# Pairing the recurrence's matmul batches and moving copies and scalings to ScalarE in a two-layer RWKV-7 / Mamba-2 / MoE kernel

## The chip, the core and the metric

The kernel runs on one core of a Trainium2 chip. The metric is the device time of one execution in microseconds (us); a lower time is better. Before the change three runs gave 3489.57 us as their median (3477.48 to 3494.5).

Engines are named as the profile names them: PE is TensorE's matmul, PEld its weight load, DVE is VectorE, ACT is ScalarE, POOL is GpSimd, SP is SyncE, which issues nearly all DMAs.

## What is computed

Two layers over 256 latent and 256 context tokens of width 1024. Each layer has a mixing block and a mixture of experts. The mixing block is one projection whose columns go to an RWKV-7 branch (16 heads of 64, scanned in both directions), a Mamba-2 branch (8 groups of 4 heads, both directions) and two gates. The two places that the change touches come from these lines of the reference:

```python
def step(S, inp):                       # RWKV-7, one token, one direction
    r_t, w_t, k_t, v_t, a_t, b_t = inp
    sa = jnp.einsum("bhij,bhj->bhi", S, a_t)
    S = S * w_t[:, :, None, :] + sa[..., None] * b_t[:, :, None, :] + v_t[..., None] * k_t[:, :, None, :]
    y = jnp.einsum("bhij,bhj->bhi", S, r_t) if emit else None
...
y = y.reshape(bsz, -1, SSM_INNER) * jax.nn.silu(z.astype(F32))     # Mamba-2, the end of a group
yg = y.reshape(bsz, -1, SSM_GROUPS, SSM_INNER // SSM_GROUPS)
yg = yg * lax.rsqrt(jnp.mean(yg * yg, axis=-1, keepdims=True) + SSM_NORM_EPS)
y = (yg.reshape(bsz, -1, SSM_INNER) * norm_w).astype(out_dtype)
```

The mixture of experts picks two of 32 experts for each token; its code is not changed.

## The kernel before

Everything that a layer does is first recorded as a list of operations. A planner inside the kernel then writes out the order in which they are issued: it keeps a clock for each engine, a price for each operation, a due time for each stream of work and a count of buffer slots, and at each step takes the operation that can start earliest, the most urgent first. What it emits is one fixed order for each engine; on the chip each engine works through its own order and waits, where an operand is not there yet, with all that stands behind. So any edit can move instructions far away from it.

The mixing block of a layer runs three kinds of streams at once: eight head pairs of the RWKV branch, eight groups of the Mamba branch, and gates. The large projections (tiles `mm` and `psz`) are split into a high and a low 16-bit half of the weights (`wh`, `wl`), which ACT and DVE make.

The RWKV recurrence is done in chunks of 64 tokens. For a head pair `i` and a direction `d`:

- `rw_dir` makes the chunk factors. `psg` holds products of keys, from which DVE masks out `QA` and `AR`. Two batches of 16 matmuls of 64x64 follow: `psat` transposes `Z`, and `psav` multiplies `QA` with the values in `SU`. ACT copies `psat` to `Z`. The two halves of `psav` go to `SU`, one by ACT, one by DVE. `Z`, `SU`, `XT` and `AR` are then written to DRAM (`sd`), because each has two slots.
- `rw_solve` inverts the triangular factors on DVE (`slW`, `slY`, `slM`) and gives `TT`; `psW` and `psZ` are its matmuls.
- `rw_chain` comes one head pair later. It reads `Z`, `SU`, `XT` and `AR` back from DRAM into the same slots and runs four batches: `psta` (`TT` times `Z`), `psua` (`TT` times `SU`), `psgt` and `psra` (with the new `Z`). Then come `psH` (state of each chunk, from `SU`, then a chain of seven steps through `GT` and `St`) and `psY` (the output).

A batch is recorded by `batch` as one operation of 16 matmuls that stay together (`together`), since they use the PE array as 64x64 tiles and other matmuls use it as 128x128. PSUM tiles of these batches come from a tag with two slots.

`ssm_group` ends with the normalisation: `yg` (128 tokens x 256 columns) is multiplied by the reciprocal root `rr` on DVE, transposed on PE into `psyT`, scaled by ACT into `yt`, and split by DVE into two 16-bit halves in `smo`, which are written to DRAM.

All instructions stand at line 683 in the profile (the planner's emitter), so they are told apart by their tiles.

Of the kernel before, what the change touches and what calls it, by code (L numbers as in the profile page):

```python
# [12 lines left out]
F32 = mybir.dt.float32  # L13
# [3 lines left out]
AF = mybir.ActivationFunctionType  # L17
OP = mybir.AluOpType
# [3 lines left out]
NT = 512  # L22
# [664 lines left out]
class Kernel:  # L687
# [469 lines left out]
    def rw_dir(self, l, i, d, S, kk, w0):  # L1157
        nc, wk, rp = self.nc, self.wk, self.rp
# [41 lines left out]
        for e in range(2):  # L1200
            rows = slice(64 * e, 64 * e + 64)
# [41 lines left out]

        rows = self.rows2
        SU = S["SU"][d]
        ps = self.batch("psat", lambda c, e: Z[rows[e], c, 0], lambda c, e: self.ident[rows[e], 64 * e:64 * e + 64])
        A.activation(Z[:, :, 0], ps, AF.Copy)
        ps = self.batch("psav", lambda c, e: QA[rows[1 - e], 2 * c + e], lambda c, e: SU[rows[1 - e], c, e])
        A.activation(SU[rows[0], :, 0], ps[rows[0]], AF.Copy)
        V.tensor_copy(SU[rows[1], :, 1], ps[rows[1]])  # L1250
        sd = self.sd[:, i, d]
        nc.sync.dma_start(sd[:, 0], Z.rearrange("p c b t -> p (c b t)"))
        nc.sync.dma_start(sd[:, 1], SU.rearrange("p c b t -> p (c b t)"))
# [7 lines left out]

    def batch(self, name, lhs, rhs, cs=range(8)):

        ps = self.psum("g", [128, 8, 64], name)
        with self.nc.together():
            for c in cs:
                for e in range(2):
                    self.nc.tensor.matmul(ps[self.rows2[e], c], lhs(c, e), rhs(c, e), start=True, stop=True)
        return ps

    def rw_solve(self, i):

# [80 lines left out]
    def rw_chain(self, l, i):  # L1353

        nc, wk, rp = self.nc, self.wk, self.rp
        V, A, T, G = nc.vector, nc.scalar, nc.tensor, nc.gpsimd
        S = self.pair[i]
        full = l == 0  # L1360
        c0 = 0 if full else 4
        o0 = 64 * c0
        E = range(2)
        rows = (slice(0, 64), slice(64, 128))
        seq = [[0, 1, 2, 3, 4, 5, 6, 7], [3, 2, 1, 0, 7, 6, 5, 4]]
        py = S["py"] = self.psum("y", [128, NT], "psY", bufs=1)
        yo = lambda c, e: py[rows[e], 64 * c - o0:64 * c - o0 + 64]
        GT = wk.tile([128, 2, 8, 64], F32, name="GT")
        St = wk.tile([128, 2, 8, 64], F32, name="St", tag="X")
        PH = []  # L1370
        batch = self.batch
        for d in range(2):
            TT = S["TT", d]
            sd = self.sd[:, i, d]
            Z = S["Z", d] = rp.tile([128, 8, 2, 64], F32, name="Z", bufs=4)
            nc.sync.dma_start(Z.rearrange("p c b t -> p (c b t)"), sd[:, 0])
            SU = rp.tile([128, 8, 2, 64], F32, name="SU", bufs=4)
            nc.sync.dma_start(SU.rearrange("p c b t -> p (c b t)"), sd[:, 1])
            XT = rp.tile([128, 8, 128], F32, name="XT", bufs=4)
            nc.sync.dma_start(XT.rearrange("p c t -> p (c t)"), sd[:, 2])  # L1380
            AR = rp.tile([128, 16, 64], F32, name="AR", bufs=4)
            nc.sync.dma_start(AR[:, 2 * c0:].rearrange("p c t -> p (c t)"), sd[:, 3, 128 * c0:])
            mid = seq[d][1:7]

            ps = batch("psta", lambda c, e: TT[rows[e], c], lambda c, e: Z[rows[e], c, 0])
            A.activation(Z[:, :, 0], ps, AF.Copy)
            ps = batch("psua", lambda c, e: TT[rows[e], c], lambda c, e: SU[rows[e], c, e])
            A.activation(SU[rows[0], :, 0], ps[rows[0]], AF.Copy)
            V.tensor_copy(SU[rows[1], :, 1], ps[rows[1]])
            ps = batch("psgt", lambda c, e: Z[rows[e], c, 0], lambda c, e: XT[rows[e], c, 64 * e:64 * e + 64], mid)  # L1390
            for cs in ((slice(0, 3), slice(5, 8)) if d else (slice(1, 7),)):
                n = cs.stop - cs.start
                V.tensor_tensor(GT[:, d, cs], ps[:, cs], self.id2[:, None, :].to_broadcast([128, n, 64]), op=OP.add)
            ph = self.psum("c", [128, 8, 64], "psH")
            PH.append(ph)
            with nc.together():
                for n, c in enumerate(seq[d][:7]):
                    for e in E:
                        T.matmul(ph[rows[e], c], XT[:, c, 64 * e:64 * e + 64], SU[:, c, e], start=n == 0, stop=False,
                                 skip_group_check=True)  # L1400
            ps = batch("psra", lambda c, e: Z[rows[e], c, 0], lambda c, e: AR[rows[e], 2 * c + e], range(c0, 8))
            V.tensor_tensor(Z[:, c0:, 1], Z[:, c0:, 1], ps[:, c0:], op=OP.add)
            with nc.together():
                for c in range(c0, 8):
                    for e in E:
                        T.matmul(yo(c, e), SU[:, c, e], AR[:, 2 * c + e], start=not d and c == c0, stop=False,
                                 skip_group_check=True)
        for n in range(7):
            cs = [seq[d][n] for d in range(2)]
            if n:  # L1410
                with nc.together():
                    for d, c in enumerate(cs):
                        for e in E:
                            T.matmul(PH[d][rows[e], c], GT[rows[e], d, c], St[rows[e], d, c], start=False, stop=True,
                                     skip_group_check=True)
            for d, c in enumerate(cs):
                nx, pl = seq[d][n + 1], S["pl", d][:, c:c + 1]
                if d:
                    A.activation(St[:, d, nx], PH[d][:, c], AF.Copy, scale=pl)
                else:  # L1420
                    V.tensor_scalar(St[:, d, nx], PH[d][:, c], pl, None, op0=OP.mult)
        with nc.together():
            for d in range(2):
                for c in range(c0, 8):
                    if c != seq[d][0]:
                        for e in E:
                            T.matmul(yo(c, e), St[rows[e], d, c], S["Z", d][rows[e], c, 1], start=False, stop=True,
                                     skip_group_check=True)
# [71 lines left out]
    def ssm_group(self, l, g):  # L1500
# [104 lines left out]
        rr = wk.tile([128, 4], F32, name="yrr", bufs=2)  # L1605
        self.rsqrt(rr[:, t0:], ss[:, t0:], 4 - t0)
        for t in range(t0, 4):
            V.tensor_scalar(yg[:, t], yg[:, t], rr[:, t:t + 1], None, op0=OP.mult)
        for b in range(2):
            pt = self.psum("t", [128, NT], "psyT")  # L1610
            for t in range(t0, 4):
                T.transpose(pt[:, 128 * t:128 * t + 128], yg[:, t, 128 * b:128 * b + 128], self.ident)
            j = 2 * g + b
            nw = self.nws[:, j:j + 1]
            yt = wk.tile([128, NT], F32, name="yt", bufs=2)
            A.activation(yt[:, o0:], pt[:, o0:], AF.Copy, scale=nw)
            o = wk.tile([128, 2, NT], F16, name="smo", bufs=2)
            V.tensor_copy(o[:, 0, o0:], yt[:, o0:])
            V.tensor_tensor(o[:, 1, o0:], yt[:, o0:], o[:, 0, o0:], op=OP.subtract)
            nc.sync.dma_start(self.smd[:, j, :, o0:], o[:, :, o0:])  # L1620


# [589 lines left out]
```

## Time and profile before

| | before |
|---|---|
| median of three runs | 3489.57 us (3477.48 to 3494.5) |
| the profiled execution | 3486.93 us |
| its span, first to last instruction | 3484.8 us |
| PE busy | 3117.4 us (89%) |
| DVE busy | 2418.7 us (69%) |
| ACT busy | 1725.3 us (50%) |
| POOL busy | 773.3 us (22%) |
| mean granted TensorE clock | 0.942 |

The page's slices show the stages: mixing of layer 0 up to 1143 us, its merge and routing, experts of layer 0 from about 1370 to 1909 us, mixing of layer 1 from there to 2848 us, merge, and experts of layer 1 to the end. The profile counts a PE that has matmuls in flight as busy, so a busy share near 90% can still hold pauses of some hundred nanoseconds. A wait is listed with the engine or DMA whose event came last before the waiting instruction started.

### The profile page before, as it was taken

The page shows a single profiled execution, that of the slowest core. Times are in us where ns is not written, and L with a number is a line of the kernel's source. Part 1 is how long each engine was busy: PE and PEld are TensorE (multiplying, and loading weights), DVE is VectorE, ACT ScalarE, POOL GpSimd, SP SyncE. Part 2 cuts the span into 40 slices and gives each one's busy share as a digit, 9 for nine tenths or more (in the row PEclk, how much of TensorE's full clock was granted, in tenths as well). Part 3 has the DMA queues.
Part 4 walks back from the last instruction along what each step waited for, and adds up shares of the span by engine and source line. Part 5 has one row for each costly group of instructions (what it writes and reads, how often), then busy time and mean ns, then how long its engine had stood idle before and what let it go on. Part 6 is the DMA issues. An engine that isn't in the chain of part 4 may idle for free. (4 is left out here: it accounts for less than half of the span.)

```text
span 3484.8 us, 84587 instructions
## 1 busy us (share of the span) xinstructions
PE 3117.4 (89%) x34930; PEld 2072.5 (59%) x34930; DVE 2418.7 (69%) x4474; ACT 1725.3 (50%) x3189; POOL 773.3 (22%) x1048
## 2 busy tenths in 40 slices
PE   6899999899889998999998698888888889898887
PEld 3556666566566457888887366566666668333332
DVE  4887877877867347999997788888887765221112
ACT  4554555544544225998886654555544443111111
POOL 1332323333332011111111243334332321000000
PEclk8999999999999997999999798999989999899998
DMA  7243463553355626999996433444234458899996
GB/s 290 91 162 133 157 215 124 199 201 126 141 183 173 249 97 242 408 390 404 394 391 256 178 108 136 150 147 151 96 140 140 156 187 304 340 401 399 401 400 259
DMA packets 283503, 794.49 MB, mean 228 GB/s; under 512 B 31457, under 2 KB 62177, under 8 KB 283105
## 3 DMA queue, kind: packets, MB, share of 16 engines
q1 hardware_dynamic: 278368, 772.17, 60.0%
q10 hardware_dynamic: 3584, 12.58, 0.9%
q8 instruction: 279, 4.57, 0.5%
q0 software_dynamic: 1152, 4.19, 0.3%
q14 instruction: 120, 0.97, 0.1%
HBM read 688.16 MB, written 100.66 MB: 226 GB/s over the span
## 5 line engine op out<-in xcount | busy, mean ns | idle before, releaser
L683 PE MATMUL mm<-h,wh 128*128 128x512 f16 (+1 forms) x2432 | 680.2, 359 | 6.4 <-ACT wh L683 6.3
L683 PEld LDWEIGHTS <-wh 128*128 128x128 f16 x3200 | 306.7, 99 | 261.4 <-issue 24.6
L683 PE MATMUL mm<-h,wl 128*128 128x512 f16 (+2 forms) x1216 | 434.4, 359 | 5.4 <-DVE wl L683 5.3
L683 DVE SCALAR_TENSOR_TENSOR ewl<-est,ewh 128x1024 f16<-128x1024 f32 x352 | 413.0, 1228 | 16.5 <-ACT ewh L683 8.1
L683 ACT ACTIVATE ewh<-est 128x1024 f16<-128x1024 f32 x384 | 380.9, 1050 | 14.1 <-PE pse L683 10.1
L683 DVE SCALAR_TENSOR_TENSOR wl<-wst,wh 128x1024 f16<-128x1024 f32 (+1 forms) x234 | 290.9, 1256 | 36.7 <-ACT wh L683 35.9
L683 PE MATMUL pse<-xg,ewh 128*128 128x96 f16 x4096 | 276.4, 206 | 4.5 <-DVE xg L683 2.1
L683 PEld LDWEIGHTS <-ewh 128*128 128x128 f16 x4096 | 265.6, 98 | 6.9 <-ACT ewh L683 0.9
L683 PE MATMUL pse<-xg,ewl 128*128 128x96 f16 x2048 | 264.4, 206 | 1.0 <-POOL ewl L683 1.0
L683 ACT ACTIVATE wh<-wst 128x1024 f16<-128x1024 f32 (+1 forms) x234 | 239.8, 1043 | 5.9 <-DMA wst<-in_wmix_dram 5.5
L683 PEld LDWEIGHTS <-wl 128*128 128x128 f16 (+1 forms) x1600 | 158.7, 99 | 137.3 <-DVE wl L683 13.0
L683 PE MATMUL pse<-est,xg 128*64 128x512 f32 x512 | 236.6, 598 | 0.0
L683 PE MATMUL pse<-esh,xg 128*64 128x512 f32 x512 | 236.6, 598 | 0.0
L683 PEld LDWEIGHTS <-ewl 128*128 128x128 f16 x2048 | 199.5, 98 | 7.4 <-issue 4.2
L683 DVE SCALAR_TENSOR_TENSOR cva<-cvz,cwh,cva 128x512 f32<-128x512 f32 (+1 forms) x256 | 199.6, 780 | 1.6
L683 POOL TENSOR_TENSOR ewl<-est,ewh 128x1024 f16<-128x1024 f32 x32 | 70.0, 2188 | 488.4 <-ACT ewh L683 429.1
L683 POOL TENSOR_TENSOR sht<-shz 128x512 f32<-128x512 f32 (+3 forms) x56 | 65.6, 1171 | 468.6 <-ACT shz L683 377.7
L683 DVE TENSOR_TENSOR slM<-slY,slW 128x144 f32<-128x144 f32 (+22 forms) x496 | 162.7, 328 | 8.3
L683 DVE SCALAR_TENSOR_TENSOR eyl<-psy,egs,eyh 128x512 f16<-128x512 f32 x32 | 24.0, 751 | 205.5 <-ACT eyh L683 205.5
L683 ACT ACTIVATE eu<-pse 128x384 f32<-128x384 f32 (+1 forms) x64 | 34.5, 540 | 243.4 <-PE pse L683 243.4
L683 DVE TENSOR_REDUCE slY<-slM 128x2 f32<-128x4 f32 (+23 forms) x496 | 147.3, 297 | 7.2
L683 PE MATMUL psz<-wh,h 128*128 128x256 f16 x768 | 150.3, 283 | 0.0
(560 smaller groups left out, 7173.6 us busy)
## 6 DMA issues: line engine op xcount, KB each, us to landing
est<-in_w_dram SPq DMA_DIRECT2D x576, 512.0 KB, 7.1
wst<-in_wmix_dram SPq DMA_DIRECT2D x246, 512.0 KB, 6.3
esh<-in_w_dram SPq DMA_DIRECT2D x384, 256.0 KB, 6.6
wst<-in_wmod_dram SPq DMA_DIRECT2D x96, 512.0 KB, 5.8
sd<-XT SPq DMA_DIRECT2D x32, 512.0 KB, 3.6
sd<-Z SPq DMA_DIRECT2D x32, 512.0 KB, 4.0
sd<-SU SPq DMA_DIRECT2D x32, 512.0 KB, 4.9
XT<-sd SPq DMA_DIRECT2D x32, 512.0 KB, 5.6
```

The lines of the kernel that those rows point to most:

```text
L683: r = getattr(e, m)(*[real(x) for x in a], **{n: real(x) for n, x in k.items()})
```

## The change

Two things are done.

1. A new helper `batches` records two batches as one operation of 32 matmuls. The pairs are `psat` with `psav`, `psta` with `psua`, and `psgt` with `psra`. The operation takes both PSUM slots at once.
2. Work goes from DVE to ACT. The second half of `psav` is copied by ACT; `yg` is scaled by ACT; ACT writes the high half of `smo` straight from `psyT`, and DVE makes the low half from `psyT` in one instruction. `yt` and the 16-bit copy on DVE are gone.

```diff
-        ps = self.batch("psat", lambda c, e: Z[rows[e], c, 0], lambda c, e: self.ident[rows[e], 64 * e:64 * e + 64])
+        ps, pu = self.batches(
+            ("psat", lambda c, e: Z[rows[e], c, 0], lambda c, e: self.ident[rows[e], 64 * e:64 * e + 64], range(8)),
+            ("psav", lambda c, e: QA[rows[1 - e], 2 * c + e], lambda c, e: SU[rows[1 - e], c, e], range(8)))
         A.activation(Z[:, :, 0], ps, AF.Copy)
-        ps = self.batch("psav", lambda c, e: QA[rows[1 - e], 2 * c + e], lambda c, e: SU[rows[1 - e], c, e])
-        A.activation(SU[rows[0], :, 0], ps[rows[0]], AF.Copy)
-        V.tensor_copy(SU[rows[1], :, 1], ps[rows[1]])
+        for e in range(2):
+            A.activation(SU[rows[e], :, e], pu[rows[e]], AF.Copy)
...
+    def batches(self, *sets):
+        out = [self.psum("g", [128, 8, 64], x[0]) for x in sets]
         with self.nc.together():
+            for ps, (_, lhs, rhs, cs) in zip(out, sets):
+                for c in cs:
+                    for e in range(2):
+                        self.nc.tensor.matmul(ps[self.rows2[e], c], lhs(c, e), rhs(c, e), start=True, stop=True)
+        return out
...
-            ps = batch("psta", lambda c, e: TT[rows[e], c], lambda c, e: Z[rows[e], c, 0])
+            ps, pu = self.batches(("psta", lambda c, e: TT[rows[e], c], lambda c, e: Z[rows[e], c, 0], range(8)),
+                                  ("psua", lambda c, e: TT[rows[e], c], lambda c, e: SU[rows[e], c, e], range(8)))
...
-            ps = batch("psgt", lambda c, e: Z[rows[e], c, 0], lambda c, e: XT[rows[e], c, 64 * e:64 * e + 64], mid)
+            ps, pr = self.batches(
+                ("psgt", lambda c, e: Z[rows[e], c, 0], lambda c, e: XT[rows[e], c, 64 * e:64 * e + 64], mid),
+                ("psra", lambda c, e: Z[rows[e], c, 0], lambda c, e: AR[rows[e], 2 * c + e], range(c0, 8)))
...
-            ps = batch("psra", lambda c, e: Z[rows[e], c, 0], lambda c, e: AR[rows[e], 2 * c + e], range(c0, 8))
...
-            V.tensor_scalar(yg[:, t], yg[:, t], rr[:, t:t + 1], None, op0=OP.mult)
+            A.activation(yg[:, t], yg[:, t], AF.Copy, scale=rr[:, t:t + 1])
...
-            yt = wk.tile([128, NT], F32, name="yt", bufs=2)
-            A.activation(yt[:, o0:], pt[:, o0:], AF.Copy, scale=nw)
             o = wk.tile([128, 2, NT], F16, name="smo", bufs=2)
-            V.tensor_copy(o[:, 0, o0:], yt[:, o0:])
-            V.tensor_tensor(o[:, 1, o0:], yt[:, o0:], o[:, 0, o0:], op=OP.subtract)
+            A.activation(o[:, 0, o0:], pt[:, o0:], AF.Copy, scale=nw)
+            V.scalar_tensor_tensor(o[:, 1, o0:], pt[:, o0:], nw, o[:, 0, o0:], op0=OP.mult, op1=OP.subtract)
```

The planner makes a new order of the whole mixing block. PE's order in the mixing block of layer 1, beside the preparation of the seventh head pair, where `psta` of the sixth starts; a row is one run of equal matmuls, `mm` are projections, `LDWEIGHTS` loads a weight tile. Before:

```order
34412 L683 MATMUL psta<-Z,TT 64x64 x16
34413 L683 MATMUL psx<-cst,X 128x128 x8
34414 L683 LDWEIGHTS wl
34415 L683 MATMUL mm<-h_30051,wl 128x256
34416 L683 MATMUL psgt<-XT,Z 64x64 x12
34417 L683 MATMUL psua<-SU,TT 64x64 x16
34418 L683 MATMUL psra<-AR,Z 64x64 x8
```

The same place in the changed kernel:

```order
34450 L683 MATMUL psta<-Z,TT 64x64 x16
34451 L683 MATMUL psua<-SU,TT 64x64 x16
34452 L683 MATMUL psat<-cst,Z 64x64 x16
34453 L683 MATMUL psav<-SU,QA 64x64 x16
34454 L683 MATMUL psH<-SU,XT 64x64 x14
34455 L683 MATMUL psY<-AR,SU 64x64 x8
34456 L683 MATMUL psgt<-XT,Z 64x64 x12
34457 L683 MATMUL psra<-AR,Z 64x64 x8
```

`psx` has moved ahead of `psta`; `psat` and `psav` of the second direction have moved up from behind `psua` of the second direction, and all eight batches now stand in one stretch of 64x64 tiles.

ACT's order at the same head pair, from the copy of `psat` of the first direction on (`wh` is a weight split, `cvt` a convolution of the Mamba branch). Before:

```order
1974 L683 ACTIVATE Z<-psat 128x8x64
1975 L683 ACTIVATE SU<-psav 64x8x64
1976 L683 ACTIVATE Z<-psta 128x8x64
1977 L683 ACTIVATE XT<-psx 128x512 x2
1978 L683 ACTIVATE SU<-psua 64x8x64
1979 L683 ACTIVATE cvt<-cva 128x512
1980 L683 ACTIVATE SU<-psua 64x8x64
```

In the changed kernel:

```order
1975 L683 ACTIVATE Z<-psat 128x8x64
1976 L683 ACTIVATE SU<-psav 64x8x64 x2
1977 L683 ACTIVATE XT<-psx 128x512 x2
1978 L683 ACTIVATE wh<-wst 128x1024
1979 L683 ACTIVATE shz<-mm 128x256
1980 L683 ACTIVATE sht<-sht,muh 128x256
1981 L683 ACTIVATE Z<-psta 128x8x64
1982 L683 ACTIVATE SU<-psua 64x8x64
1983 L683 ACTIVATE Z<-psat 128x8x64
1984 L683 ACTIVATE SU<-psav 64x8x64 x2
```

ACT has the second copy of `psav` too, and other work now stands between these copies and those of `psta` and `psua`.

## Rows read from the trace of the kernel before

**Rows 1.** Windows, mixing of layers 0 and 1: stretch, length, busy us by engine.

```profile
core 0: us, PE busy (x) PEld busy (x) DVE busy (x) ACT busy (x) POOL busy (x), PEclk, DMA share, GB/s
60.00:1143.00 1083.00, 997.54 (x11166) 646.74 (x11162) 847.23 (x1724) 549.60 (x1213) 340.02 (x483) 0.97 0.45 160
...
1909.00:2848.00 939.00, 794.45 (x9216) 575.11 (x9216) 766.46 (x1631) 490.27 (x1049) 307.00 (x481) 0.91 0.41 141
```

**Rows 2.** Timeline of PE near 300 us: start, length, instruction, tiles, count.

```profile
300.31 0.38 PE L683 MATMUL mm<-h,wh 128*128 128x512 f16 x1
300.62 0.45 PE L683 MATMUL psH<-St,GT 64*64 64x64 f32 x8
301.00 0.39 PE L683 MATMUL mm<-h,wl 128*128 128x512 f16 x1
301.23 0.59 PE L683 MATMUL mm<-h,wh 128*128 128x512 f16 x2
```

**Rows 3.** Timeline, layer 1, seventh head pair: a batch pair, its write and reload.

```profile
2644.09 0.97 PE L683 MATMUL psat<-cst,Z 64*64 64x64 f32 x26
...
2645.93 0.39 PE L683 MATMUL mm<-h,wh 128*128 128x256 f16 x2
...
2646.82 0.58 ACT L683 ACTIVATE SU<-psav 64x512 f32<-64x512 f32 x1
...
2647.45 0.37 SPq L683 DMA_DIRECT2D sd<-Z  x1
...
2647.88 0.42 SPq L683 DMA_DIRECT2D Z<-sd  x1
...
2648.39 0.99 SPq L683 DMA_DIRECT2D sd<-SU  x1
...
2649.43 0.47 SPq L683 DMA_DIRECT2D SU<-sd  x1
...
2654.06 1.98 PE L683 MATMUL psta<-Z,TT 64*64 64x64 f32 x32 [3.81 <-DMA Z<-sd]
```

**Rows 4.** Windows: the stretch that begins with that `psta`.

```profile
2653.50:2660.30 6.80, 6.24 (x83) 5.74 (x85) 1.50 (x4) 1.69 (x3) 0.00 (x0) 0.50 0.49 196
```

**Rows 5.** Groups of DVE by form: count, busy us, mean ns, idle before.

```profile
L683 DVE SCALAR_TENSOR_TENSOR eyl<-psy,egs,eyh 128x512 f16<-128x512 f32 x32 | 24.0, 751 | 205.5 <-ACT eyh L683 205.5
...
L683 DVE COPY SU<-psav 64x512 f32<-64x512 f32 x32 | 22.2, 694 | 7.3 <-PE psav L683 3.3 <-ACT SU L683 3.1
L683 DVE TENSOR_SCALAR yg<-yg,yrr 128x256 f32<-128x256 f32 x48 | 14.7, 355 | 9.3 <-POOL yrr L683 9.3
...
L683 DVE TENSOR_TENSOR smo<-yt,smo 128x512 f16<-128x512 f32 x16 | 11.7, 732 | 0.3
...
L683 DVE CAST smo<-yt 128x512 f16<-128x512 f32 x16 | 6.8, 426 | 27.0 <-ACT yt L683 27.0
L683 DVE CAST smo<-yt 128x256 f16<-128x256 f32 x16 | 6.6, 411 | 2.9 <-ACT yt L683 2.7
```

**Rows 6.** Groups of ACT by form, the same columns.

```profile
L683 ACT ACTIVATE St<-psH,pl 128x64 f32<-128x64 f32 x112 | 35.3, 316 | 109.0 <-PE psH L683 108.9
L683 ACT ACTIVATE zz<-yg 128x256 f32<-128x256 f32 x48 | 20.1, 418 | 31.5 <-DVE yg L683 29.8 <-DVE st L683 1.4
...
L683 ACT ACTIVATE SU<-psav 64x512 f32<-64x512 f32 x32 | 18.7, 585 | 15.4 <-PE psav L683 13.3 <-DVE SU L683 2.0
```

**Rows 7.** Groups of PE that wait for the batches' operands, the same columns.

```profile
L683 PE MATMUL psta<-Z,TT 64*64 64x64 f32 x1024 | 43.9, 244 | 23.7 <-DMA Z<-sd 22.6 <-DVE Sst L683 0.5 <-issue 0.4
...
L683 PE MATMUL psua<-SU,TT 64*64 64x64 f32 x1024 | 40.3, 235 | 14.8 <-DMA SU<-sd 12.5 <-DVE slM L683 1.7 <-DVE cva L683 0.4
...
L683 PE MATMUL psH<-SU,XT 128*64 128x64 f32 x896 | 36.8, 226 | 11.6 <-DVE SU L683 7.5 <-ACT SU L683 4.1
```

**Rows 8.** DMA issues: tiles, count, KB each, median us to landing.

```profile
Z<-sd SPq DMA_DIRECT2D x32, 512.0 KB, 6.2
SU<-sd SPq DMA_DIRECT2D x32, 512.0 KB, 7.2
```

More of the change, by code (lines that the diff above doesn't have):

```diff
@@ L1262, in batch @@
     def batch(self, name, lhs, rhs, cs=range(8)):
-        ps = self.psum("g", [128, 8, 64], name)
+        return self.batches((name, lhs, rhs, cs))[0]
+    def batches(self, *sets):
+        out = [self.psum("g", [128, 8, 64], x[0]) for x in sets]
         with self.nc.together():
[L1266 to L1269, printed above, removed]
+            for ps, (_, lhs, rhs, cs) in zip(out, sets):
[3 more added lines that the diff above has]
+        return out
     def rw_solve(self, i):
@@ L1370, in rw_chain @@
         PH = []
-        batch = self.batch
         for d in range(2):
@@ L1383, in rw_chain @@
             mid = seq[d][1:7]
-            ps = batch("psta", lambda c, e: TT[rows[e], c], lambda c, e: Z[rows[e], c, 0])
+            ps, pu = self.batches(("psta", lambda c, e: TT[rows[e], c], lambda c, e: Z[rows[e], c, 0], range(8)),
+                                  ("psua", lambda c, e: TT[rows[e], c], lambda c, e: SU[rows[e], c, e], range(8)))
             A.activation(Z[:, :, 0], ps, AF.Copy)
-            ps = batch("psua", lambda c, e: TT[rows[e], c], lambda c, e: SU[rows[e], c, e])
-            A.activation(SU[rows[0], :, 0], ps[rows[0]], AF.Copy)
-            V.tensor_copy(SU[rows[1], :, 1], ps[rows[1]])
-            ps = batch("psgt", lambda c, e: Z[rows[e], c, 0], lambda c, e: XT[rows[e], c, 64 * e:64 * e + 64], mid)
+            A.activation(SU[rows[0], :, 0], pu[rows[0]], AF.Copy)
+            V.tensor_copy(SU[rows[1], :, 1], pu[rows[1]])
+            ps, pr = self.batches(
+                ("psgt", lambda c, e: Z[rows[e], c, 0], lambda c, e: XT[rows[e], c, 64 * e:64 * e + 64], mid),
+                ("psra", lambda c, e: Z[rows[e], c, 0], lambda c, e: AR[rows[e], 2 * c + e], range(c0, 8)))
             for cs in ((slice(0, 3), slice(5, 8)) if d else (slice(1, 7),)):
@@ L1400, in rw_chain @@
                                  skip_group_check=True)
-            ps = batch("psra", lambda c, e: Z[rows[e], c, 0], lambda c, e: AR[rows[e], 2 * c + e], range(c0, 8))
-            V.tensor_tensor(Z[:, c0:, 1], Z[:, c0:, 1], ps[:, c0:], op=OP.add)
+            V.tensor_tensor(Z[:, c0:, 1], Z[:, c0:, 1], pr[:, c0:], op=OP.add)
             with nc.together():
```

## The prediction

> **What bounds the kernel now.** I read the windows by stage first. The edits lie in the mixing blocks alone, which fill 1083 and 939 us of the span [rows 1]; the experts and merges have other code, and I leave them as they are. In the mixing of layer 0 PE is busy 997.5 of 1083 us (92%) and DVE 847.2 (78%): PE sets the pace and only some 85 us of its idle time can be won. In layer 1 PE is busy 794.5 of 939 us (85%) and DVE 766.5 (82%): neither engine is full, both run through fixed orders, and each waits for the other, so that relief of DVE can show there. ACT is busy for 51% and 52% and POOL for about a third. The granted clock is 0.97 and 0.91, so layer 1 also spends a part of its time at the lower of the two levels, 1.2 GHz.
>
> Then I read one place. In layer 1, PE ran out of work and waited 3.81 us for the reload of `Z` before `psta` [rows 3]. The stretch that began with that `psta` had a granted clock of 0.50, the 1.2 GHz level, for 6.8 us [rows 4]. So a stall of some microseconds costs its own length and then about half of the next 6.8 us. Over the whole kernel PE idled 23.7 us before `psta`, 14.8 before `psua` and 11.6 before `psH` on its first inputs, 50.1 us together, nearly all for the two reloads and the two copies into `SU` [rows 7].
>
> **Fewer changes of the array's tiling.** Pairing lets the planner put 64x64 batches next to each other. Counted over PE's whole order up to the merges, neighbours of unlike tile size fall from 469 to 441 in layer 0 and from 327 to 272 in layer 1: 83 changes, 41 round trips. The price of a trip: from one 512-column `mm` to the next are 0.23 us (301.00 to 301.23), with a step of `psH` between them 0.69 us (300.31 to 301.00), so that step costs 0.46 us for its 8 records [rows 2]. In a long stretch `psat` and `psav` take 2645.93 - 2644.09 = 1.84 us for 64 records, 0.23 us for 8 [rows 3]. The difference, 0.23 us, is a round trip. 41 x 0.23 = 9 us, on PE and so on the path: **-9 us**. The trip is the same whatever else happens; only the count could mislead, where a change fell into an idle moment (bounds 0 and -9).
>
> Not all pairs are new. Before, `psat` and `psav` were already neighbours 26 times of 32, `psgt` and `psra` 22 times, `psta` and `psua` 3 times. So the change of order is mostly in the last pair, and the trips come from there.
>
> **Work off DVE.** Away go 32 copies of `psav` (22.2 us), 48 scalings of `yg` (14.7 us) and 32 casts (6.8 and 6.6 us): 50.3 us [rows 5]. The subtraction turns from two SBUF operands into one from PSUM with a scale; the nearest row is `eyl`, 751 ns against 732 ns for the subtraction now, so that is free. By layer: layer 0 has 16 copies, 32 scalings and the wide casts, 11.1 + 9.8 + 6.8 = 27.7 us; layer 1 the remaining 22.6 us. How much comes through lies between nothing (DVE's idle time just grows) and all 50.3 us. For layer 0 I take a fifth, 6 us, since PE is 92% busy there; for layer 1 half, 11 us, as PE and DVE are almost equally loaded. **-17 us**.
>
> **Work onto ACT.** 32 copies of 585 ns are 18.7 us. The scaling of `yg` has no row; `zz<-yg`, the same 128x256 with SBUF on both sides, takes 418 ns, `St<-psH` with a scale per partition but 64 columns 316 ns [rows 6]. I take 418 ns, the row of the same size: 48 x 0.418 = 20 us. The write of `smo` takes the place of that of `yt`. So ACT has 39 us more on top of 550 and 490 us [rows 1]. It idles half of the time, which hides most of it. Not hidden is where a copy is waited for: `SU` of `psav` was done by two engines side by side and now by one, 585 ns later; who waits is the write `sd<-SU`, but that stood behind `sd<-Z` and `Z<-sd` on SP's queue until 2648.39, 1 us after ACT's copy had ended at 2647.40 [rows 3]. I take **+4 us**, between 0 and 39.
>
> Here a rule speaks against the change. `yg` costs 355 ns on DVE and by the nearest row 418 ns on ACT [rows 5, 6], so in engine time the move loses. The Trainium skill's page "ScalarE: Activation LUTs", section "Rules for kernel authors", says that multiplications and the like belong on VectorE, not on ScalarE, since VectorE does them faster per element. The trace agrees on the price and by that rule this term would be a loss; what it leaves out is that DVE is the fuller engine here.
>
> **The pairs' own waits.** A pair is placed where both inputs are there. `psH` used to stand right behind `psua`, `psra` or a few projections; now, at the place shown from the order, `psat` and `psav` lie between (1.84 us [rows 3]) and a copy takes 585 to 694 ns [rows 5, 6]. I take half of the 11.6 us: **-6 us**. The reloads can go both ways. `psua` now follows `psta` at once, so PE waits for the later of `Z` and `SU`: `SU<-sd` is issued 1.55 us after `Z<-sd` [rows 3] and takes 7.2 us against 6.2 [rows 8], some 2.5 us later. Against that the planner has put more in front: at the place of the 3.81 us stall the order has 26 projections, two halves of `psg` and the `psx` set between `psav` and `psta`, before 17 projections and one half. The bounds are the whole 35 us of waits for reloads (22.6 + 12.5 [rows 7]) won, and 32 x 2.5 = 80 us lost; I take **0**.
>
> **Sum.** -9 - 17 + 4 - 6 = -28 us. The profiled execution took 3486.93 us (span 3484.8 us and 2.1 us around it), so 3459 us; the median of the runs is 2.6 us above it, so 3462 us. A measurement of this kernel tells about 0.5% from no change, 17 us: faster is below 3472 us, slower above 3507 us.
>
> **Rivals.**
>
> *PE has no room, and DVE's relief stays slack.* For it: 92% busy in layer 0, and the waits that the edits touch are 50.1 us in both layers [rows 7], of some 230 us in which PE idles in the two mixing blocks [rows 1]. Then only the trips and ACT's 4 us remain: 3490 - 9 + 4 = 3485 us, no change. Chance 0.26.
>
> *Slower: the pair waits for `SU`.* PE's order is fixed, so `psta` and all projections behind `psua` stand until `SU` has landed. For it: the two reloads go through one queue, one behind the other [rows 3]. Against it: more work in front. It decides from the point where the work between `psav` and `psua` is shorter than the way of `SU` through DRAM: from the end of its copy at 2647.40 to 2649.43 + 7.2 = 2656.6, some 9 us. If half of the 32 places fall short by 2.5 us, that is 40 us, and if every second of those brings 6.8 us at half clock, 8 x 3.4 = 27 us more: 3490 + 67 - 28 = 3529 us. Chance 0.15.
>
> *Slower: ACT's copies come too late.* As a mechanism of this kernel: ACT's queue is in order, so `Z<-psta` stands behind the scalings and PE stands at `psgt`; all 39 us on the path and DVE's relief lost gives 3490 - 9 - 6 + 39 = 3514 us. For it: `Z<-psta` now has a weight split and two shifts ahead of it. Against it: ACT is idle half of the time. This is the outcome of the rule on ScalarE cited above. Chance 0.05.
>
> *Much faster: the stalls fall together.* All 50.3 us off DVE count, the 9 us of trips, 12 us of waits before `psH` and a third of the reloads' 35, without stretches at half clock behind them: 3490 - 83 = 3407 us. For it: the clock of 0.91 in layer 1. Chance 0.12.
>
> **How the numbers follow.** My forecast, 3462 us, has 0.42. Faster is forecast and much faster, 0.54; the same 0.26; slower 0.20. The likeliest case alone spans 3435 to 3472 us. The range for 8 in 10 must take in no change and parts of both tails: 3415 to 3515 us.
>
> **What would show it.** Layer 0's mixing, which ends with the first `psbr`, should be about 12 us shorter than now, and layer 1's some 16 us shorter than 939 us [rows 1]. DVE should be about 28 and 23 us less busy in the two stretches, ACT some 20 us more in each. The idle time before `psta` should stay near 24 us with `psua` near zero, and that before `psH` halve. If `psua` shows long waits for `SU<-sd`, the second rival is right; if ACT's copy of `psta` ends `psgt`'s waits, the third. Wrong altogether would be the sum if unrelated waits (projections for their weights, `pscw` for the decay) change by more than these terms, because the planner has moved everything.

## The result, and the profile after the change

Six runs of the changed kernel gave a median of 3442.36 us (3439.25 to 3446.36); six runs of the kernel before beside them 3484.45 us. The ratio is 0.9879 [0.9865, 0.9893]: **42 us faster**, where 28 us were forecast. The profiled execution took 3439.67 us (span 3437.7 us, mean granted clock 0.942, as before).

By stage, with the first `psbr` as the end of a mixing block:

| stage, us | before | after | difference | forecast |
|---|---|---|---|---|
| to the first `psbr` of layer 0 | 1143.7 | 1125.3 | -18.4 | -12 |
| merge and routing, layer 0 | 226.1 | 217.5 | -8.6 | |
| experts, layer 0 | 530.4 | 529.9 | -0.5 | |
| mixing, layer 1 | 947.6 | 924.2 | -23.4 | -16 |
| merge, layer 1 | 133.0 | 133.6 | +0.6 | |
| experts, layer 1 | 504.1 | 507.1 | +3.0 | |

The 8.6 us of the first merge belong at least in part to the mixing before it: the trace has 11551 matmuls ahead of the first `psbr` now and 1221 in the merge, where it had 11471 and 1299, so some 80 were brought forward. Nothing else moved by more than 3 us.

Windows of the kernel after, one for each mixing block (start and end, length, busy time and instructions of PE, PEld, DVE, ACT, POOL, granted clock, DMA share, GB/s); they answer to [rows 1]:

```profile
60.00:1125.00 1065.00, 990.74 (x11242) 646.89 (x11240) 826.35 (x1662) 570.76 (x1262) 346.06 (x481) 0.97 0.46 165
1882.00:2797.00 915.00, 785.18 (x9199) 574.19 (x9200) 738.89 (x1584) 507.56 (x1078) 295.04 (x481) 0.90 0.42 146
```

The length less PE's busy time is PE's idle time: 74 and 130 us, against 85 and 145 before. DVE has 21 and 28 us less to do, ACT 21 and 17 us more. The clock stayed where it was.

The groups of the edited instructions and of those that wait for them (busy us, mean ns, idle us before them and what ended it):

```profile
L683 PE MATMUL psua<-SU,TT 64*64 64x64 f32 x1024 | 39.9, 232 | 10.7 <-DMA SU<-sd 10.5
L683 PE MATMUL psta<-Z,TT 64*64 64x64 f32 x1024 | 39.8, 230 | 10.6 <-DMA Z<-sd 9.4 <-ACT xT L683 0.7 <-POOL rwq L683 0.4
L683 ACT ACTIVATE SU<-psav 64x512 f32<-64x512 f32 x64 | 37.6, 588 | 2.4 <-PE psav L683 1.9
...
L683 PE MATMUL psH<-SU,XT 128*64 128x64 f32 x896 | 35.2, 229 | 7.4 <-ACT SU L683 5.3 <-DVE SU L683 1.9
...
L683 DVE COPY SU<-psua 64x512 f32<-64x512 f32 x32 | 22.2, 695 | 13.6 <-PE psua L683 8.4 <-ACT SU L683 3.2 <-DMA wst<-in_wmix_dram 1.3
...
L683 ACT ACTIVATE yg<-yg,yrr 128x256 f32<-128x256 f32 x48 | 20.9, 497 | 11.3 <-POOL yrr L683 11.3
```

Against [rows 7], the idle time before `psta` fell from 23.7 to 10.6 us, before `psua` from 14.8 to 10.7, before `psH` from 11.6 to 7.4. The scaling of `yg` costs ACT 497 ns, more than the 418 ns assumed from [rows 6]. DVE's new subtraction costs what was assumed from [rows 5]:

```profile
L683 DVE SCALAR_TENSOR_TENSOR smo<-psyT,nws,smo 128x512 f16<-128x512 f32 x16 | 12.0, 750 | 48.7 <-ACT smo L683 48.7
```

Last, what PE waits for from the first mixing block to the second merge (us in total, times, longest us):

```profile
PE psW L683 <- DVE slO L683: 25.5, 10, 4.2
PE pstr L683 <- DVE rmss L683: 21.2, 1, 21.2
PE psx L683 <- POOL X L683: 16.5, 8, 3.0
PE pscw L683 <- ACT lp L683: 11.9, 8, 3.2
PE pspos L683 <- DVE at L683: 11.1, 1, 11.1
PE psua L683 <- DMA SU<-sd: 10.5, 9, 2.7
PE psx L683 <- DVE X L683: 10.5, 8, 2.6
```

The reload of `Z`, the longest wait before the change (22.6 us), is gone from the top, and the longest now is for DVE's triangular solve (`slO`): 25.5 us, where the same row had 12.9 us before:

```profile
PE psW L683 <- DVE slO L683: 12.9, 7, 2.6
```

### The profile page after: what moved, and what is told of

Read it like the earlier page. It is cut to its first block, busy times and chain, and to the rows that moved or that the text cites. A ratio compares the mean times of both kernels' runs of the same rounds, so it can differ in the third digit from the quotient of the medians.

```text
span 3437.7 us, 84603 instructions
## 1 busy us (share of the span) xinstructions
PE 3098.2 (90%) x34930; PEld 2068.0 (60%) x34930; DVE 2371.8 (69%) x4362; ACT 1762.4 (51%) x3269; POOL 768.1 (22%) x1048
## 3 DMA queue, kind: packets, MB, share of 16 engines
q1 hardware_dynamic: 278368, 772.17, 60.6%
## 5 line engine op out<-in xcount | busy, mean ns | idle before, releaser
L683 POOL TENSOR_TENSOR rmsr<-rmss,mhalf 128x1 f32<-128x1 f32 x16 | 12.7, 793 | 576.3 <-DVE rmss L683 568.4
```

Source lines behind the costliest of these rows:

```text
L683: r = getattr(e, m)(*[real(x) for x in a], **{n: real(x) for n, x in k.items()})
```

## The experiments

The times are medians of several runs beside runs of the kernel before on the same chip; the ratio is to that kernel (its medians were 3484 to 3487 us). Two such medians differ by chance by some 7 us, as the intervals show. "After" is the changed kernel, 3442 us.

### Which half of the change counts

The moves to ACT alone, in the order that the planner makes of them:

```diff
-        V.tensor_copy(SU[rows[1], :, 1], ps[rows[1]])
+        A.activation(SU[rows[1], :, 1], ps[rows[1]], AF.Copy)
...
-            V.tensor_scalar(yg[:, t], yg[:, t], rr[:, t:t + 1], None, op0=OP.mult)
+            A.activation(yg[:, t], yg[:, t], AF.Copy, scale=rr[:, t:t + 1])
...
-            A.activation(yt[:, o0:], pt[:, o0:], AF.Copy, scale=nw)
             o = wk.tile([128, 2, NT], F16, name="smo", bufs=2)
-            V.tensor_copy(o[:, 0, o0:], yt[:, o0:])
-            V.tensor_tensor(o[:, 1, o0:], yt[:, o0:], o[:, 0, o0:], op=OP.subtract)
+            A.activation(o[:, 0, o0:], pt[:, o0:], AF.Copy, scale=nw)
+            V.scalar_tensor_tensor(o[:, 1, o0:], pt[:, o0:], nw, o[:, 0, o0:], op0=OP.mult, op1=OP.subtract)
```

> The moves from VectorE to ScalarE alone, no pairs; the planner makes its own order. Before is 3484 us and the changed kernel 3442 us here, 42 us apart. Theory of the sum (relief of DVE and fewer tiling trips are separate terms): relief and ScalarE's extra work were -13 of -28 us, so about half of the 42 us shows: some 3464 us, with 50 us less DVE time and 39 us more ACT time. Rival, the pairs are all of it: 3480 to 3488 us. Rival, the relief is all of it: 3440 to 3448 us.

Measured: 3455.81 us, 0.991 [0.9893, 0.9928], so -30 us: more than the sum said (3464), less than the rival in which the relief is all of it.

The three pairs alone: the changed kernel with these lines turned back.

```diff
-        for e in range(2):
-            A.activation(SU[rows[e], :, e], pu[rows[e]], AF.Copy)
+        A.activation(SU[rows[0], :, 0], pu[rows[0]], AF.Copy)
+        V.tensor_copy(SU[rows[1], :, 1], pu[rows[1]])
...
-            A.activation(yg[:, t], yg[:, t], AF.Copy, scale=rr[:, t:t + 1])
+            V.tensor_scalar(yg[:, t], yg[:, t], rr[:, t:t + 1], None, op0=OP.mult)
...
```

> The three pairs alone, with the copies, scalings and casts on VectorE as before. Theory of the sum: trips and waits before psH were -15 of -28 us, so some 3464 us; PE's tiling changes in the mixing blocks are 713 here too (432 + 281), which at 0.23 us a round trip is 9 us. Rival, the pairs are all of it: 3440 to 3448 us. Rival, the relief is all of it: 3480 to 3488 us.

Measured: 3480.44 us, 0.9977 [0.9966, 0.9989], so -5 us by the medians and -8 us by the ratio. The moves bring the larger part; with both the gain is 42 us, not far from the sum of the two, 35 to 38 us. That both also change the order is the trouble with these two runs, and the reason for the next two.

### The engine or the order

An added field lets the planner price an instruction on one engine while it is issued on the other at the same place, so that order and engine can be changed apart. The copies of `psav` and the scalings of `yg` are treated so; `smo` stays as it is in the kernel taken as base. The order of before, with the work on ACT:

```diff
-                e = getattr(nc, o.eng)
-                for m, a, k in o.calls:
+                e = getattr(nc, o.alt[0] if o.alt else o.eng)
+                for m, a, k in [o.alt[1:]] if o.alt else o.calls:
...
+        nc.alt = "scalar", "activation", (SU[rows[1], :, 1], ps[rows[1]], AF.Copy), {}
         V.tensor_copy(SU[rows[1], :, 1], ps[rows[1]])
...
+            nc.alt = "scalar", "activation", (yg[:, t], yg[:, t], AF.Copy), dict(scale=rr[:, t:t + 1])
             V.tensor_scalar(yg[:, t], yg[:, t], rr[:, t:t + 1], None, op0=OP.mult)
```

> The order of the kernel before, word for word on TensorE, but at the places of the 32 copies of psav and the 48 scalings of yg the instruction is issued on ScalarE instead of VectorE (37 us off DVE; the split into smo stays). Theory of direct relief: DVE gets on earlier wherever it is waited for, some 10 us: 3470 to 3478 us. Rival, the gain comes only with a new order, since each engine's order is fixed and the others wait for other things: 3481 to 3490 us.

Measured: 3478.93 us, 0.9987 [0.9972, 1.0002]. The interval reaches no change, though 37 us (22.2 + 14.7 of [rows 5]) have left DVE.

The order of after, with that work back on DVE (the same field, with "vector" in place of "scalar"):

> The order of the changed kernel, word for word on TensorE, but the second copies of psav and the scalings of yg are issued on VectorE at the places where ScalarE had them (37 us back on DVE). Theory of direct relief: some 10 to 15 us of the gain go, 3452 to 3457 us. Rival, the order is what counts: 3440 to 3447 us.

Measured: 3470.85 us, 0.9963 [0.9948, 0.9979]: 28 us over the changed kernel for 37 us put back, more than either expectation allowed. So the same 37 us are worth 28 us in the new order and 6 us or nothing in the old one. **What the relief of DVE is worth depends on the order**, and in the old one hardly any of it arrived. That instructions behind a removed one start earlier only as far as their other operands are there is the likely reason; it was not traced to places.

### What an engine's time is worth: PE

Into the changed kernel, between the halves of every pair, goes a one-column matmul that uses the array as 128x128 (its result is overwritten by the batch that follows). That adds 96 round trips between the tilings, over twice the 41 that the prediction counted as saved; the order of everything else stays.

```diff
+                w = None
                 for m, a, k in o.calls:
+                    if o.fn and w not in (None, a[0].tensor.name) and tiles[w].name in ("psat", "psta", "psgt"):
+                        x = real(a[0])
+                        nc.tensor.matmul(bass.AP(tensor=x.tensor, offset=0, ap=[[x.ap[0][0], 128], [1, 1]]),
+                                         self.spare[:, 0:128], self.spare[:, 0:1], start=True, stop=True)
+                    w = a[0].tensor.name if o.fn else None
...
```

> The changed kernel, its order kept, with a one-column 128x128 matmul (its result is overwritten) between the two batches of each pair: 96 more round trips of the array's tiling. At 0.23 us a trip plus some 0.06 us for the matmul itself: +22 to +28 us over the changed kernel's 3442 us, so 3464 to 3470 us. Rival, the trips fall where PE waits anyway: 3442 to 3450 us. Rival, breaking the stretch costs more than the trip: over 3475 us.

The trips were really paid for. Timeline of PE (start, length, instruction, tiles, count) at one pair of `psat` and `psav`, after:

```profile
2603.45 0.97 PE L683 MATMUL psat<-cst,Z 64*64 64x64 f32 x26
...
2604.38 0.98 PE L683 MATMUL psav<-SU,QA 64*64 64x64 f32 x27
2605.29 0.39 PE L683 MATMUL mm<-h,wh 128*128 128x256 f16 x2
```

and the same pair with the extra trip:

```profile
2605.33 1.15 PE L689 MATMUL psat<-cst,Z 64*64 64x64 f32 x32
2606.41 0.18 PE L686 MATMUL psav<-tri 128*128 128x1 f16 x1
2606.52 1.15 PE L689 MATMUL psav<-SU,QA 64*64 64x64 f32 x32
2607.60 0.39 PE L689 MATMUL mm<-h,wh 128*128 128x256 f16 x2
```

From the start of `psat` to the projection behind the pair it is 1.84 us without and 2.27 us with the extra matmul, 0.43 us for one. The other two kinds of pairs pay less. `psgt` with `psra`, after and then with the extra trip:

```profile
2620.69 0.91 PE L683 MATMUL psgt<-XT,Z 64*64 64x64 f32 x24
...
2622.00 0.39 PE L683 MATMUL mm<-h,wh 128*128 128x512 f16 x1
```

```profile
2625.02 0.91 PE L689 MATMUL psgt<-XT,Z 64*64 64x64 f32 x24
...
2626.59 0.39 PE L689 MATMUL mm<-h,wh 128*128 128x512 f16 x1
```

That is 1.31 and 1.57 us. Over all pairs of a kind the median difference is 0.43 us for `psat` with `psav` and 0.25 us for each of the other two, so the 96 trips are some 30 us by estimate (32 x 0.93); 0.43 us for all of them would be 41 us, the figure that the next expectation uses. Measured: **3442.10 us**, 0.9881 [0.9866, 0.9896], the time of the changed kernel. Its windows:

```profile
60.00:1128.00 1068.00, 1002.03 (x11293) 654.71 (x11295) 821.98 (x1662) 570.57 (x1262) 347.17 (x483) 0.97 0.46 164
1886.00:2802.00 916.00, 793.63 (x9249) 580.58 (x9247) 741.04 (x1584) 507.83 (x1079) 295.73 (x481) 0.91 0.42 146
```

PE is 20 us busier in the two together and idles 16 us less (66 and 122 us instead of 74 and 130): at 93% busy it still had room.

### What an engine's time is worth: DVE and ACT

Into the order of after go small additions on DVE, four behind each ACT copy of `psat` and `psta` in the program, with a scratch tile as output, so that nothing waits for them but what stands behind on DVE.

```diff
+                if o.eng == "scalar" and isinstance(a[1], bass.AP) and a[1].tensor.name in tiles:
+                    v = tiles[a[1].tensor.name].name
+                    if v == "psat" or v == "psta":
+                        s = self.spare[:, 0:64]
+                        for _ in range(4):
+                            nc.vector.tensor_tensor(self.junk, s, s, op=OP.add)
...
```

> The changed kernel, its order kept; at each of the 64 copies of psat and psta VectorE also does four small additions (128x64, into a scratch tile that nobody reads), some 36 us in all. 41 us more work on TensorE had cost nothing (the extra trips). If VectorE is what paces the mixing blocks: 3465 to 3478 us. If no engine paces it, and the waits between them do: 3442 to 3455 us.

The group of the additions and the windows:

```profile
L689 DVE TENSOR_TENSOR junk<-cst 128x64 f32<-128x64 f32 x256 | 79.4, 310 | 6.7
```

```profile
60.00:1156.00 1096.00, 1000.67 (x11244) 654.48 (x11241) 854.92 (x1790) 570.57 (x1262) 343.49 (x481) 0.96 0.45 160
1915.00:2860.00 945.00, 797.77 (x9201) 585.01 (x9201) 767.25 (x1712) 508.35 (x1079) 290.72 (x481) 0.89 0.41 142
```

Measured: 3502.99 us, 1.0056 [1.0035, 1.0076], **61 us over the changed kernel**. That is above both ranges on record, and the additions cost more than I had put there: 79.4 us by their own records, 56 us of DVE's busy time (2371.8 to 2427.8 us). Counted over both traces, the other DVE instructions have 16 us less in their records, `X<-b,Pi` above all (67.4 to 60.5 us), and records overlap with their neighbours by 7 us more. So in this order a us of DVE's busy time costs about one us (60.6 / 56.0 = 1.08), and as much in layer 0 as in layer 1: the windows are 31 and 30 us longer than after. The run with the copies and scalings put back on DVE has the same price: 28.5 us for 26.2 us of busy time (2371.8 to 2398.0), 1.09.

The additions also show where an instruction of DVE gets longer. Four of them take 1.00 us at one place and 3.96 us at another, where POOL works beside them:

```profile
132.27 3.08 POOL L683 TENSOR_TENSOR X<-th,Pi 64x512 f32<-64x512 f32 x2
...
132.83 3.96 DVE L689 TENSOR_TENSOR junk<-cst 128x64 f32<-128x64 f32 x4
...
404.41 1.00 DVE L689 TENSOR_TENSOR junk<-cst 128x64 f32<-128x64 f32 x4
```

Of the 256 additions 32 took longer than 0.4 us, and each of these has a POOL instruction beside it for more than half of its time; of the other 224 only 16 have.

The same at the same places on ACT, three copies each:

```diff
-                        for _ in range(4):
-                            nc.vector.tensor_tensor(self.junk, s, s, op=OP.add)
+                        for _ in range(3):
+                            nc.scalar.activation(self.junk, s, AF.Copy)
```

> The changed kernel, its order kept; at each of the 64 copies of psat and psta ScalarE also does three small copies (128x64, into a scratch tile that nobody reads), some 38 us in all. If ScalarE has room, as its busy share of about 52% says: 3442 to 3450 us. If what counts is how soon its copies come: 3455 to 3480 us.

```profile
L689 ACT ACTIVATE junk<-cst 128x64 f32<-128x64 f32 x192 | 48.9, 255 | 4.3
```

```profile
60.00:1122.00 1062.00, 990.68 (x11245) 646.83 (x11244) 822.58 (x1662) 592.05 (x1359) 347.59 (x481) 0.97 0.46 165
1880.00:2795.00 915.00, 785.31 (x9201) 574.98 (x9201) 739.07 (x1584) 528.03 (x1175) 293.75 (x481) 0.90 0.42 146
```

Measured: 3443.40 us, 0.9885 [0.9867, 0.9904]. ACT is 42 us busier in the two windows and nothing is lost, although the copies stand right ahead of those into `SU`. **Of the three engines that were loaded only DVE passes added work on to the end**, while it is 78 and 81% busy and PE 93 and 86%. Whether it is DVE's load as a whole that does it or a chain of dependent steps that runs through DVE these runs do not tell apart; for ACT the same places were harmless. POOL, a third of the time busy, was not loaded, so a part that it plays beside DVE is not ruled out.

### Where the pairs come in

Only the pair of the chain's first two batches (`psta` with `psua`), on top of the moves to ACT; `psat`, `psav`, `psgt` and `psra` go each by themselves:

```diff
-            ps = batch("psta", lambda c, e: TT[rows[e], c], lambda c, e: Z[rows[e], c, 0])
+            ps, pu = self.batches(("psta", lambda c, e: TT[rows[e], c], lambda c, e: Z[rows[e], c, 0], range(8)),
+                                  ("psua", lambda c, e: TT[rows[e], c], lambda c, e: SU[rows[e], c, e], range(8)))
```

> The moves to ScalarE and psta with psua as the only pair. 464 + 296 = 760 tiling changes against 787 with no pair (3456 us) and 713 with all (3442 us): by the number of trips 3450 to 3453 us. If this pair is what the pairs give: 3442 to 3446 us. If its wait for SU costs: 3457 us or more.

Measured: 3462.08 us, 0.9939 [0.9924, 0.9954]. And the changed kernel without that pair:

```diff
-            ps, pu = self.batches(("psta", lambda c, e: TT[rows[e], c], lambda c, e: Z[rows[e], c, 0], range(8)),
-                                  ("psua", lambda c, e: TT[rows[e], c], lambda c, e: SU[rows[e], c, e], range(8)))
+            ps = self.batch("psta", lambda c, e: TT[rows[e], c], lambda c, e: Z[rows[e], c, 0])
...
+            pu = self.batch("psua", lambda c, e: TT[rows[e], c], lambda c, e: SU[rows[e], c, e])
```

> The changed kernel with psta and psua as single batches again, the other two pairs kept. TensorE's tiling changes are then 456 + 333 = 789 instead of 713, 38 round trips more, 9 us: 3451 us by the sum. If the pair's wait for the reload of SU had cost something, this one wins it back: below 3440 us. If the pairs do nothing: 3440 to 3445 us.

Measured: 3471.03 us, 0.9966 [0.9953, 0.9979]. With the moves to ACT in all four, no pair gives 3456 us, one 3462, the two others 3471 and all three 3442. The 6 us between the first two are within what medians differ by chance; the two other pairs lose 15 us and the whole wins 13, which no sum of prices explains: each of the four has an order of its own over the whole block. The expectations don't explain it either: 3471 us lies in none of the three ranges, and 3462 us in that for a pair whose wait for `SU` costs, but there `psua` waits 7.8 us and `psta` 2.6, where they wait 5.2 and 17.6 us without a pair. What all four have in common is DVE's list of instructions, 4362 of them, and yet DVE's busy time differs: 2375.9, 2387.0, 2393.0 and 2371.8 us, named in the same order. The instructions are the same and some take longer. In the changed kernel:

```profile
L683 DVE SCALAR_TENSOR_TENSOR cva<-cvz,cwh,cva 128x512 f32<-128x512 f32 x224 | 179.8, 803 | 1.9
L683 DVE TENSOR_SCALAR cva<-cvz,cwh,cbh 128x512 f32<-128x512 f32 x56 | 34.6, 617 | 3.3 <-ACT cvz L683 1.9 <-issue 1.2
L683 DVE TENSOR_TENSOR E<-E 128x512 f32<-128x512 f32 x48 | 33.4, 698 | 3.4 <-ACT E L683 3.3
```

and without the pair of `psta` and `psua`:

```profile
L683 DVE SCALAR_TENSOR_TENSOR cva<-cvz,cwh,cva 128x512 f32<-128x512 f32 x224 | 184.4, 823 | 1.7
L683 DVE TENSOR_SCALAR cva<-cvz,cwh,cbh 128x512 f32<-128x512 f32 x56 | 37.7, 674 | 2.8 <-ACT cvz L683 2.3
L683 DVE TENSOR_TENSOR E<-E 128x512 f32<-128x512 f32 x48 | 36.0, 750 | 2.9 <-ACT E L683 2.8
```

What the longer ones meet is POOL again. In the changed kernel 160 of the 224 `cva` in the rows above have no POOL instruction beside them and take 744 ns, 756 at most; the other 64 take 950 ns on average. Without the pair it is 73, and they take 991 ns.

DVE's time is not the whole answer. The profiled executions took 3461.22 (no pair), 3457.97, 3460.52 and 3439.67 us (all pairs), so 4, 15 and 21 us more of DVE's time go with 22, 18 and 21 us more in all. The largest of PE's waits in the three slower kernels is for `X`, of which POOL and DVE each make a part, and is ended by POOL. In the order named it is

```profile
PE psx L683 <- POOL X L683: 38.6, 15, 5.8
...
PE psx L683 <- POOL X L683: 37.2, 13, 5.8
...
PE psx L683 <- POOL X L683: 45.3, 16, 5.0
```

where the changed kernel has 16.5 us. It would be enough for the difference, but no run tried whether this wait reaches the end, and what the pairs are worth by themselves **stays open**.

### Two tries beyond the change

If DVE paces, its other half copy, of `psua`, should go to ACT as well:

```diff
-            V.tensor_copy(SU[rows[1], :, 1], pu[rows[1]])
+            A.activation(SU[rows[1], :, 1], pu[rows[1]], AF.Copy)
```

> The changed kernel with the second copy of psua on ScalarE too: another 22 us off DVE and 19 us onto ACT. If relief of DVE with a new order goes on paying as it did in the moves alone (30 us for 50): 3430 us. If ScalarE's copies now come too late for psH, where both are waited for: 3445 to 3455 us.

Measured: **3398.71 us**, 0.9761 [0.9744, 0.9778], the best of all, 44 us below the changed kernel for 22 us of DVE, and 31 us below what was expected. Windows and groups:

```profile
60.00:1108.00 1048.00, 985.15 (x11259) 643.61 (x11256) 812.49 (x1646) 582.36 (x1281) 352.54 (x483) 0.98 0.47 168
1867.00:2756.00 889.00, 771.87 (x9201) 561.41 (x9199) 733.33 (x1568) 517.51 (x1095) 304.40 (x481) 0.92 0.43 150
```

```profile
L683 PE MATMUL psta<-Z,TT 64*64 64x64 f32 x1024 | 39.1, 229 | 1.0 <-DMA Z<-sd 0.9
L683 ACT ACTIVATE SU<-psua 64x512 f32<-64x512 f32 x64 | 37.7, 590 | 14.0 <-PE psua L683 12.7 <-ACT Z L683 0.5
...
L683 PE MATMUL psua<-SU,TT 64*64 64x64 f32 x1024 | 37.3, 224 | 5.7 <-DMA SU<-sd 4.9 <-DVE slY L683 0.9
...
L683 PE MATMUL psH<-SU,XT 128*64 128x64 f32 x896 | 34.2, 226 | 0.6 <-ACT SU L683 0.4 <-issue 0.2
```

The waits that the change was about are nearly gone (1.0, 5.7 and 0.6 us), and PE idles 63 and 117 us. The same edit in the order of after, by the field used above:

> The changed kernel's order, but the second copy of psua is issued on ScalarE at the place where VectorE had it. With a new order the same move gave 3399 us. If the relief itself does it: 3400 to 3415 us. If the planner's new order does it, as with the first moves (4 us in the old order, 30 us in a new one): 3430 to 3442 us.

Measured: 3431.09 us, 0.9848 [0.9828, 0.9867], so -11 us; the other 32 us of the best kernel come with its new order. The pattern is that of the moves before: part of it at the place, more once the order is made anew. Whether a new order gains because of the relief or is by chance a better one these runs do not tell.

The last takes the first tap of the Mamba convolution, 64 instructions, from DVE to ACT on top of the best kernel:

```diff
-        V.tensor_scalar(a, z[:, :nseg, 0:256], w(0), self.cbh[:, b:b + 1], op0=OP.mult, op1=OP.add)
+        A.activation(a, z[:, :nseg, 0:256], AF.Identity, scale=w(0), bias=self.cbh[:, b:b + 1])
```

> The kernel with psua's copy on ScalarE (3399 us), and the convolution's first tap, 64 instructions of 655 ns, moved from VectorE to ScalarE as well, with a new order. If relief of VectorE goes on paying: 3365 to 3385 us. If ScalarE has become the fuller engine or the tap is waited for: 3395 to 3420 us.

Measured: 3419.32 us, 0.9815 [0.9791, 0.984], 21 us worse than its base. The first mixing block came out 5.5 us shorter (1107.6 to 1102.1 us), the second 19.5 us longer (898.2 to 917.7). DVE's busy time fell by only 18 us (2351.9 to 2333.9), where the taps had 38 us in their records (34.8 and 3.2). The other taps, which now start from ACT's output, wait for it. They take 833 ns instead of 812; 87 of the 224 now stand beside a POOL instruction where 75 did, and the rest take 744 and 742 ns:

```profile
L683 DVE SCALAR_TENSOR_TENSOR cva<-cvz,cwh,cva 128x512 f32<-128x512 f32 x224 | 186.6, 833 | 7.1 <-ACT cva L683 4.9 <-issue 0.8
```

A chain of five steps on one engine became a chain over two. The waits for ACT's `cva`, in this row and in that of the 256-column form (4.9 us each), are some 10 us; the rest of the loss lies in the order of layer 1 and was not traced to a place.

## Why the prediction was right in sum and wrong in its parts

**The sum.** Forecast -28 us, measured -42. The likeliest case, that some of DVE's relief comes through, is the one that came; but it got there by other terms than those written down, and that the time fell inside its 3435 to 3472 us is in part luck. What is shown is that 28 of the 42 us hang on the copies and scalings being on ACT in the new order; how the rest divides between the order, `smo` and the pairs is open.

**Tiling trips, -9 us: this step failed.** It counted 41 trips of 0.23 us "on PE and so on the path". The price of one is real, 0.25 us at two kinds of pairs and 0.43 at the third, so it isn't "the same whatever else happens" either; but the path is not PE's: 96 more trips, some 30 us, changed the time by nothing. Of the bounds given, the other one, 0, was the right end. The Trainium skill's page "TensorEngine Tiling (Array Packing)", section "Key Properties", says that a change of tiling mode drains TensorE; the timeline with the extra matmul agrees that a round trip costs time there (0.25 and 0.43 us), and the run says that here nobody waited for it.

**"PE sets the pace" in layer 0: failed, and with it the split of DVE's relief.** The step took a fifth of the relief in layer 0 because PE was 92% busy, and half in layer 1. A share of 92% left 85 us idle, and the extra trips showed that PE takes more without loss. DVE, at 78%, passes on all of what is added. The term of -17 us was mis-sized: the moves alone measured -30 us for 50.3 us, and in the fixed order of after 37 us of them were worth 28. DVE's busy time was forecast to fall by 28 and 23 us in the two windows and fell by 21 and 28.

**ACT, +4 us: the price was mis-sized, the cover was right.** The scaling takes 497 ns and not 418, so ACT got some 4 us more than reckoned; but 49 us more of it, at the places of other copies, cost nothing, so the term is about 0.

**The rule against the change.** `yg` costs 355 ns on DVE [rows 5] and 497 ns on ACT, so in engine time the move loses. The Trainium skill's "ScalarE: Activation LUTs", section "Rules for kernel authors", sends multiplications to VectorE; the advantage that it names is for bf16 and operations of one source, and the 355 and 497 ns here, in fp32, point the same way. The time went the other way: in the order of after a us more of DVE costs about a us and 49 us more of ACT nothing. The rival built on it (3514 us) did not come about; its sign, `psgt` waiting for ACT's `Z`, stayed at 0.9 us in all (2.1 before).

**The waits.** `psH` was forecast to halve and went from 11.6 to 7.4 us: -4 instead of -6. The reload waits were taken as 0, with a stay at 24 us before `psta` and almost none before `psua`; they measured 10.6 and 10.7, so 17 us less together. The rival in which the pair waits for `SU` lost: `psua` does wait for `SU<-sd`, but for less than before. Either half of the change shortens them, the moves alone (first two lines) by 16 us and the pairs alone (last two) by 28.5:

```profile
L683 PE MATMUL psta<-Z,TT 64*64 64x64 f32 x1024 | 39.9, 229 | 17.6 <-DMA Z<-sd 16.4 <-ACT TT L683 0.5 <-issue 0.4
...
L683 PE MATMUL psua<-SU,TT 64*64 64x64 f32 x1024 | 38.5, 228 | 5.2 <-DMA SU<-sd 5.2
```

```profile
L683 PE MATMUL psta<-Z,TT 64*64 64x64 f32 x1024 | 39.4, 227 | 6.5 <-DMA Z<-sd 5.0 <-POOL rwq L683 1.1 <-POOL xe L683 0.4
L683 PE MATMUL psua<-SU,TT 64*64 64x64 f32 x1024 | 38.1, 226 | 3.5 <-DMA SU<-sd 3.1 <-DVE xc L683 0.3
```

With the pairs alone that went with only 5 to 8 us of time, so these waits were not worth their length there and the 17 us can't be added to DVE's relief. The extra trips say the same of PE's time at these places, and the wait for DVE's `slO` grew (12.9 to 25.5 us).

**The rival of no change** rested on PE having no room, and fell with that reading. It would have been right for the old order: with 37 us off DVE and the order kept, the time hardly moved (-6 us, with an interval that reaches 0). **The stage lengths** forecast as -12 and -16 us measured -18.4 and -23.4, in the proportion forecast, which was luck as the reasons for it fell.

## What to carry to other kernels

The fullest engine need not be the one that paces: put some tens of us of independent work into each engine's fixed order and see which the end follows. Take work from that engine, even at a worse price per instruction elsewhere, and try it with a new order too, since with the order kept only a part of the relief arrived here (6 of 37 us, 11 of 22). Where a planner remakes the order, a single variant says little about an edit, since four pairings of the same work lay 29 us apart here.

## What the runs showed that I had not expected

- A small matmul of another tiling between two batches costs PE 0.25 or 0.43 us at its place, and 96 of them nothing at the end.
- DVE instructions of one form have no fixed duration: `cva` took 803 or 823 ns and `E<-E` 698 or 750 ns in two kernels whose DVE instructions are the same and stand in another order. In the traces the long ones are those beside a POOL instruction: no `cva` of that size without one takes over 756 ns in either. No run moved POOL's work to see what that is worth at the end.
- Work added to DVE raises its busy time by less than its own records: 79.4 us of additions raised it by 56 us, since other DVE instructions came out 16 us shorter, with fewer of them beside POOL's (41 of the 64 `X<-b,Pi` instead of 50), and records overlapped by 7 us more. The sum of a group's records is then not what the engine gives up.
- On ACT, a 128x256 scaling with SBUF on both sides and a scale per partition takes 497 ns, 79 ns more than `zz<-yg` of the same size [rows 6], which has no scale from a tile but squares and sums; the two differ in more than the scale, so its share is not shown.
